# A two-layer diffusion block on one core: more buffers and an earlier load around the third stage, and the modulation beside Hyena and the second MLP moved from ScalarE and GpSimd to VectorE, its loads from SyncE's queue to GpSimd's

## The chip, the core and the metric

The kernel runs on one core of a Trainium2 chip. The metric is the device time of one execution in microseconds (us). TensorE (PE) multiplies, VectorE (DVE) and ScalarE (ACT) work on tiles elementwise, GpSimd (POOL) does a few elementwise operations and issues some DMAs, and SyncE (SP) issues the other DMAs. Each engine runs its own instructions in the order in which they stand in the program.

## The reference, cut to what matters

A block of two layers on 256 latent and 256 context tokens of 2048 channels, in float32. Layer 0 mixes tokens with a bidirectional RWKV-7 scan, layer 1 with a Hyena long convolution; each is followed by an MLP of width 8192. Six vectors a layer, made from the condition `c`, shift, scale and gate the streams. They are the modulation, and each is a matrix of 2048 x 2048 times a vector:

```python
mod = (silu_c @ ada_w[i] + ada_b[i]).reshape(B, N_MOD, 1, D)      # i = layer
h = modulate(rms_norm(x, norm_g[i, 0]), mod[:, 0], mod[:, 1])
y = rwkv_mixer(...)  if kind == 0 else  hyena_stream(h, ...)
x = x + mod[:, 2] * rms_norm(y, norm_g[i, 1])
h = modulate(rms_norm(x, norm_g[i, 2]), mod[:, 3], mod[:, 4])
x = x + mod[:, 5] * rms_norm(squared_relu_mlp(h, mlp_up[i], mlp_down[i]), norm_g[i, 3])
```

All of both layers' `ada_w` has to be loaded, 201 MB of float32, and the kernel spreads that over its stages.

## The kernel before, in words

**Precision.** A float32 operand is split into a high part (`wh`, `xh`: a cast on ACT) and a low part (`wl`, `xl`: a subtraction on DVE), and `mm3` makes three matmuls of them. A weight block of 1 MB is loaded by SP's queue into `w`, and each half of it costs one `wh` cast on ACT and one `wl` subtraction on DVE (`load_split`, `split_into`).

**Stages, in order of time.** (1) `start`, to 172 us: the first modulation and the mixes of the context and latent streams. (2) `rwkv_proj`, to about 440: the key projection `w_k`, with the second halves of the low-rank nets (`lora2`) beside it. After each block of keys `evk` copies it out (`kt`), squares it (`ksq`), splits the square (`ksh`, `ksl`) and sums it by heads on PE (line 783). (3) `rwkv_begin`, about 440 to 556, the third stage: the rest of `lora2`, `fill_r` and `fill_v` (projections of r and v, whose inputs `fx` are loaded by GpSimd's queue), and `scan_prepare(0)`, which makes the first scan group's operands (`KB`, `ard`, `Mn`, then an inversion in 31 pairs of `tmp` and `d`). (4) `rwkv_scan`, to about 1399. (5) `rwkv_out`, to 1475. (6) the first MLP, to 2245. (7) `hyena`, to about 2842: 24 pairs of column blocks of `hy_in_w` in the transposed layout, with `spectral` (transforms by matmul: `ud`, `pa`, `pb`, `ph`, `pl`) of one quarter of the channels beside the projections of the next, then `hy_out_w`, whose rows are evacuated as `y` and summed as `ysq`, and `resid`, which needs the factor `dg`. (8) the second MLP, to the end.

**`lora2`** makes 80 tiles in stages 2 and 3: three matmuls into `sc`, a tanh by ACT into `l2t`, a scaling of `l2t` by DVE or GpSimd, for 32 of them a scan by DVE into `l2u`, and a store of `l2t` or `l2u` to `scr` (`cum`, `a`, `gate`) by SP. A new `l2t` or `l2u` waits until the store of the tile that had its buffer has landed. In stage 3 its pool holds 3 buffers of each.

**The modulation.** `ada_first` and `ada_scan` put the vector through PE. `ada_run`, used in stages 2, 6, 7 and 8, multiplies a block of 128 rows by a scalar a row and adds it up: `acc += aw * s`, 16 blocks for 512 columns, then a matmul with `ones` and a small addition (`reduce`). The table `ONP` says for each stage which engines do it: with False, one DVE operation a block (`scalar_tensor_tensor`); with True, ACT scales `aw` in place and GpSimd adds it to `acc`. `ADA` says how many pieces of 512 columns a stage has: 16 in the first MLP, 8 in Hyena, 4 in the second MLP. A load `aw` holds one block beside Hyena (256 KB) and two beside the MLPs (512 KB), with two buffers; all of them are issued by SP. `ada_scan` loads its first `aw` when the scan begins.

**What sets the order.** The kernel is written as generators that take turns (`tick`, `beside`), and a scheduler of the framework then places each instruction by priority and by its own estimate of times; `high_priority` moves instructions ahead. So an edit can change the order on every engine. Pools set when a buffer is free again.

Of the kernel before, what the change touches and what calls it, by code (L numbers as in the profile page):

```python
# [10 lines left out]
F32 = mybir.dt.float32  # L11
F32R = mybir.dt.float32r
BF16 = mybir.dt.bfloat16
AF = mybir.ActivationFunctionType
# [55 lines left out]
class Kern:  # L70
# [233 lines left out]

    def ada_run(self, n, pool, psum="mm", on_pool=True, per=2, bufs=2, behind=None):


        nc = self.nc

        def reduce(layer, ch, i, acc):  # L310
            ps = getattr(self, psum).tile([P, 4, 2], F32, name=psum)
            for b in range(4):
                nc.tensor.matmul(ps[:, b, :], lhsT=acc[:, b * P : (b + 1) * P], rhs=self.ones[:, 0:2], start=True, stop=True)
            nc.vector.tensor_tensor(self.mod[:, layer, ch, 4 * i : 4 * i + 4], ps[:, :, 0],
                                    self.col("ada_b", layer * 96 + ch * 16 + 4 * i, 4), op=ALU.add)

        last = None
        for layer, ch, i in itertools.islice(self.ada_todo, n):
            acc = pool.tile([P, 512], F32, name="acc", bufs=per)
            c0 = ch * D + i * 512  # L320
            for k in range(0, KT, per):
                w = pool.tile([P, per, 512], F32, name="aw", bufs=bufs)
                with self.tc.issue_after(behind) if behind else ExitStack():
                    nc.sync.dma_start(w, self.I["ada_w"][layer, k * P : (k + per) * P, c0 : c0 + 512].rearrange("(a p) n -> p a n", p=P))
                for a in range(per):
                    s = self.sc2[:, 0, k + a : k + a + 1]
                    if on_pool:
                        nc.scalar.activation(w[:, a] if k + a else acc, w[:, a], AF.Identity, scale=s)
                        if k + a:
                            nc.gpsimd.tensor_tensor(acc, acc, w[:, a], op=ALU.add)  # L330
                    elif k + a == 0:
                        nc.vector.tensor_scalar(acc, w[:, a], s, None, op0=ALU.mult)
                    else:
                        nc.vector.scalar_tensor_tensor(acc, w[:, a], s, acc, op0=ALU.mult, op1=ALU.add)
                if k == 4 and per == 2 and last:
                    reduce(*last)
                yield
            last = layer, ch, i, acc
            if per == 1:
                yield  # L340
                reduce(*last)
        yield
        yield
        if last and per == 2:
            reduce(*last)

    def ada_scan(self, n, pool):
# [11 lines left out]
        todo = [(layer, ch, i, half, k4) for layer, ch, i in itertools.islice(self.ada_todo, n) for half in range(2) for k4 in range(4)]  # L359

        def load(u):
            layer, ch, i, half, k4 = todo[u]
            w = pool.tile([P, 4, 256], F32, name="aw", bufs=2)
            c0 = ch * D + i * 512 + half * 256
            nc.sync.dma_start(w, self.I["ada_w"][layer, k4 * 512 : (k4 + 1) * 512, c0 : c0 + 256].rearrange("(a p) n -> p a n", p=P))
            return w

        def finish(layer, ch, i, half, ps):
# [8 lines left out]

        nxt = load(0)
        tail = iter(())
# [16 lines left out]

    ONP = (False, False, False, True, True)
    ADA = (4, 8, 16, 8, 4)
# [298 lines left out]
    def lora2(self, pool):  # L697
# [33 lines left out]
        for q in range(4):  # L731
            for nm, e in (("dec", 0), ("dec", 1), ("a", 0), ("a", 1)):
                b0 = self.hw0 if nm == "dec" else self.ha0
                w = next(block)
                for j in range(4):
                    m = 4 * q + j
                    ps = self.sc.tile([P, 512], F32, name="sc")
                    self.mm3(ps, self.cut(w, slice(j * P, (j + 1) * P)), self.lora[nm, e], True, True)
                    t = self.l2p[0].tile([P, 512], F32, name="l2t")
                    nc.scalar.activation(t, ps, AF.Tanh, scale=0.5, bias=b0[:, e * 16 + m : e * 16 + m + 1])  # L740
                    (nc.gpsimd if m % 4 < self.LPOOL else nc.vector).tensor_scalar(t, t, 0.5, 0.5, op0=ALU.mult, op1=ALU.add)
                    if nm == "dec":
                        u = self.l2p[0].tile([P, 512], F32, name="l2u")
                        s = slice(None, None, -1 if e else 1)
# [4 lines left out]
        for q in range(8):  # L749
            w = next(block)  # L750
            for j in range(2):
                m = 2 * q + j
                ps = self.sc.tile([P, 512], F32, name="sc")
                for k in range(2):
                    self.mm3(ps[:, :L], self.cut(w, slice(k * 256 + j * P, k * 256 + (j + 1) * P)), self.lora["g", k], k == 0, k == 1)
                t = self.l2p[0].tile([P, 512], F32, name="l2t")
                nc.scalar.copy(t[:, :L], ps[:, :L])
# [3 lines left out]
    def rwkv_proj(self, l2, ad1):  # L761
# [11 lines left out]
        def evk(m, ps):  # L773
# [5 lines left out]
            sl = ev.tile([P, 512], F32R, name="ksl", bufs=1)  # L779
            nc.scalar.activation(s, ps, AF.Square, scale=self.col("k_k", m))  # L780
            self.split_into(sh[:], s[:], sl[:])
            for x in (sh, sl):
# [194 lines left out]
    def rwkv_scan(self, es, prep_pools, ngroups=KT // 2):  # L977
# [12 lines left out]
        ada = self.ada_scan(self.ADA[1], pool("ad", 2))  # L990
        self.bg, self.rate = [], 0.0
        with self.tc.high_priority(self.PRS):
            for i in range(2):
                self.scan_values(0, i)
# [749 lines left out]
    def run(self):  # L1744
        nc, tc = self.nc, self.tc
        with ExitStack() as es:
# [28 lines left out]
            with ExitStack() as e1:  # L1775
# [7 lines left out]
                for i, phase in enumerate((lambda: self.mlp(x, 0), lambda: self.hyena(x, (), 0), lambda: self.mlp(x, 1))):  # L1783
                    if self.upto >= 3 + i:
                        with ExitStack() as e2:
                            if self.ADA[2 + i]:
                                ad = self.pool(e2, "ad")
                                per = 1 if i == 1 else 2
                                ada = self.ada_run(self.ADA[2 + i], ad, "sg", self.ONP[2 + i], per)
                                if i == 1:  # L1790
# [97 lines left out]
```

## Time and profile before

| what | us |
|---|---|
| median of 3 runs (3551.66 to 3564.56) | 3557.94 |
| the profiled execution's own time | 3560.04 |
| its span, first to last instruction | 3558.3 |
| PE busy in the span | 3310.4 (93%) |
| DVE, ACT, POOL busy | 2453.0, 1749.9, 436.7 |

The page's chain of work that ended last follows back from the last instruction what released it. In the table by stretch, "PE busy" says how much of a stretch at least one matmul was in flight; since matmuls overlap, a stretch with PE busy for all of it has no wait left on PE. A wait names the instruction that waited, what ended the wait, the total in us, the count and the longest.

### The profile page before, as it was taken

The page shows a single profiled execution, that of the slowest core. Times are in us where ns is not written, and L with a number is a line of the kernel's source. Part 1 is how long each engine was busy: PE and PEld are TensorE (multiplying, and loading weights), DVE is VectorE, ACT ScalarE, POOL GpSimd, SP SyncE. Part 2 cuts the span into 40 slices and gives each one's busy share as a digit, 9 for nine tenths or more (in the row PEclk, how much of TensorE's full clock was granted, in tenths as well). Part 3 has the DMA queues.
Part 4 walks back from the last instruction along what each step waited for, and adds up shares of the span by engine and source line. Part 5 has one row for each costly group of instructions (what it writes and reads, how often), then busy time and mean ns, then how long its engine had stood idle before and what let it go on. Part 6 is the DMA issues. An engine that isn't in the chain of part 4 may idle for free.

```text
span 3558.3 us, 74568 instructions
## 1 busy us (share of the span) xinstructions
PE 3310.4 (93%) x30598; PEld 2894.7 (81%) x30598; DVE 2453.0 (69%) x3867; ACT 1749.9 (49%) x3070; POOL 436.7 (12%) x496
## 2 busy tenths in 40 slices
PE   6899888999899888899999999999999899999999
PEld 3477677887788766798989898899887798989897
DVE  4688776777777755687877776678786675555554
ACT  4454454555445444454444445566564663444343
POOL 0011121111111000000000002044441540000000
PEclk9899999999999989999999999999999999999999
DMA  9668898998888735688888886477665775555553
GB/s 309 203 224 285 261 343 271 290 282 262 259 268 262 227 122 186 201 272 280 284 296 281 298 265 228 160 224 227 213 204 179 241 256 189 178 189 189 189 180 129
DMA packets 587807, 836.79 MB, mean 235 GB/s; under 512 B 39551, under 2 KB 373280, under 8 KB 587464
## 3 DMA queue, kind: packets, MB, share of 16 engines
q1 hardware_dynamic: 556360, 718.76, 62.8%
q0 software_dynamic: 31104, 113.26, 10.2%
q8 instruction: 239, 3.92, 0.4%
q14 instruction: 104, 0.85, 0.1%
HBM read 777.31 MB, written 54.59 MB: 234 GB/s over the span
## 4 chain that ended last, share of the span: by engine, by line
PE 60%; DMA 16%; DVE 11%; ACT 5%; issue 4%; POOL 2%; SPq 1%; ACTq 0%; DVEq 0%; POOLq 0%
PE mm L112 45%; DMA aw<-in_ada_w 9%; PE sg L112 5%; PE fl L112 5%; PE sc L112 4%; POOL acc L330 2%; DVE tmp L53 1%; DVE wl L53 1%; DVE d L53 1%; ACT aw L53 1%; ACT wh L53 1%; DMA win<-in_window 1%; PE sc L414 1%; DMA cum<-cum 1%; PE sg L460 1%
## 5 line engine op out<-in xcount | busy, mean ns | idle before, releaser
L53 DVE TENSOR_TENSOR wl<-w,wh 128x1024 fp32r<-128x1024 f32 (+1 forms) x716 | 916.7, 1283 | 487.5 <-ACT wh L53 483.3
L53 ACT CAST wh<-w 128x1024 fp32r<-128x1024 f32 (+1 forms) x716 | 745.8, 1044 | 642.6 <-PE mm L112 578.7
L112 PE MATMUL mm<-hxh,wh 128*128 128x258 f32 x2816 | 801.1, 286 | 3.3 <-DVE nt L53 2.6
L112 PE MATMUL mm<-hxh,wl 128*128 128x258 f32 x2816 | 798.7, 284 | 3.8 <-DVE wl L53 3.6
L112 PE MATMUL mm<-hxl,wh 128*128 128x258 f32 x2816 | 797.9, 284 | 0.0
L112 PEld LDWEIGHTS mm<-hxh,wl 128*128 128x128 f32 x2816 | 532.3, 189 | 6.3 <-DVE wl L53 5.0
L112 PEld LDWEIGHTS mm<-hxh,wh 128*128 128x128 f32 x2816 | 532.8, 190 | 5.4 <-DVE nt L53 2.9
L112 PEld LDWEIGHTS mm<-hxl,wh 128*128 128x128 f32 x2816 | 535.1, 190 | 2.0 <-DVE hxl L53 0.2
L330 POOL TENSOR_TENSOR acc<-acc,aw 128x512 f32<-128x512 f32 x180 | 277.3, 1540 | 1325.9 <-PE mm L112 960.4
L112 PE MATMUL mm<-wh,uh 128*128 128x512 f32 x1024 | 403.0, 394 | 0.0
L112 PE MATMUL mm<-wh,ul 128*128 128x512 f32 x1024 | 401.0, 392 | 0.0
L112 PE MATMUL mm<-wl,uh 128*128 128x512 f32 x1024 | 398.5, 389 | 0.0
L53 DVE SCALAR_TENSOR_TENSOR acc<-aw,sc,acc 128x512 f32<-128x512 f32 x300 | 224.9, 750 | 98.6 <-DMA aw<-in_ada_w 96.1
L112 PEld LDWEIGHTS mm<-wh,ul 128*128 128x128 f32 x1024 | 192.1, 188 | 43.9
L112 PEld LDWEIGHTS mm<-wl,uh 128*128 128x128 f32 x1024 | 192.3, 188 | 41.8
L112 PE MATMUL fl<-fh,fx 128*128 128x256 f32 x1024 | 215.5, 297 | 11.3 <-DMA fx<-xv 9.8
L112 PEld LDWEIGHTS mm<-wh,uh 128*128 128x128 f32 x1024 | 192.4, 188 | 39.4
L53 ACT ACTIVATE aw<-aw,sc 128x512 f32<-128x512 f32 x180 | 125.9, 719 | 147.1 <-DMA aw<-in_ada_w 143.9
L112 PEld LDWEIGHTS fl<-fh,fx 128*128 128x128 f32 x1024 | 169.3, 194 | 29.0 <-issue 13.0
L112 PE MATMUL fl<-flo,fx 128*128 128x256 f32 x512 | 146.5, 286 | 0.0
L112 PE MATMUL sg<-ard,KB 64*64 64x64 f32 (+1 forms) x3584 | 130.5, 245 | 12.0 <-DVE NT L53 3.7
L112 PEld LDWEIGHTS sg<-ard,KB 64*64 64x64 f32 x3584 | 111.5, 137 | 18.3 <-DVE NT L53 4.7
(361 smaller groups left out, 5879.9 us busy)
## 6 DMA issues: line engine op xcount, KB each, us to landing
aw<-in_ada_w SPq DMA_DIRECT2D x288, 512.0 KB, 5.9
w<-in_mlp_down SPq DMA_DIRECT2D x128, 1024.0 KB, 5.3
w<-in_mlp_up SPq DMA_DIRECT2D x120, 1024.0 KB, 6.2
fx<-xv POOLq DMA_DIRECT2D x128, 512.0 KB, 6.3
aw<-in_ada_w SPq DMA_DIRECT2D x192, 256.0 KB, 3.7
w<-in_hy_in_w SPq DMA_DIRECT2D x44, 1024.0 KB, 5.3
fx<-xr POOLq DMA_DIRECT2D x64, 512.0 KB, 5.7
w<-in_w_k SPq DMA_DIRECT2D x16, 1024.0 KB, 7.7
```

Source lines behind the costliest of these rows:

```text
L53: return self.kern.pin(self.key, f(*a, **kw))
L112: return self.pin("pe", self.nc.tensor.matmul(out, lhsT=lhsT, rhs=rhs, **kw))
L330: nc.gpsimd.tensor_tensor(acc, acc, w[:, a], op=ALU.add)
L414: nc.tensor.matmul(ps[:, :n], lhsT=self.ones, rhs=sq[:, :n], start=acc is None and k == 0, stop=k == len(x) - 1)
L460: nc.tensor.matmul(pt[:, s], lhsT=y[k // 4, tt][:, k % 4 * P : (k % 4 + 1) * P], rhs=dg[:, tt], start=True, stop=True)
```

## The change

Five things change. `ada_scan` is cut in two, and its first `aw` load is issued when the scan's other pools are opened, at high priority, instead of after the scan's first values. `lora2`'s `l2t` gets 6 buffers and `l2u` 4 in stage 3, for 3 each (in stage 2 both keep 2). In `evk` the square and split of the last two key blocks get high priority. `ONP` becomes False for Hyena and the second MLP, so DVE does there what ACT and GpSimd did. In the same two stages the loads of `aw` are issued by GpSimd's queue.

```diff
-    def ada_run(self, n, pool, psum="mm", on_pool=True, per=2, bufs=2, behind=None):
+    def ada_run(self, n, pool, psum="mm", on_pool=True, per=2, bufs=2, behind=None, queue=None):
...
-                    nc.sync.dma_start(w, self.I["ada_w"][layer, k * P : (k + per) * P, c0 : c0 + 512].rearrange("(a p) n -> p a n", p=P))
+                    (queue or nc.sync).dma_start(w, self.I["ada_w"][layer, k * P : (k + per) * P, c0 : c0 + 512].rearrange("(a p) n -> p a n", p=P))
...
+        return self.ada_steps(pool, wide, pick, todo)
+
+    def ada_steps(self, pool, wide, pick, todo):
+        nc = self.nc
+
...
+        with self.tc.high_priority(self.PRS):
+            first = load(0)
+        yield
...
-        nxt = load(0)
+        nxt = first
...
-    ONP = (False, False, False, True, True)
+    ONP = (False, False, False, False, False)
...
-                    t = self.l2p[0].tile([P, 512], F32, name="l2t")
+                    t = self.l2p[0].tile([P, 512], F32, name="l2t", bufs=2 * self.l2p[1] + 2 * (self.l2p[1] > 1))
...
-                        u = self.l2p[0].tile([P, 512], F32, name="l2u")
+                        u = self.l2p[0].tile([P, 512], F32, name="l2u", bufs=2 * self.l2p[1])
...
-            nc.scalar.activation(s, ps, AF.Square, scale=self.col("k_k", m))
-            self.split_into(sh[:], s[:], sl[:])
+            with self.tc.high_priority(self.PRS if m >= KT - 2 else 0):
+                nc.scalar.activation(s, ps, AF.Square, scale=self.col("k_k", m))
+                self.split_into(sh[:], s[:], sl[:])
...
         ada = self.ada_scan(self.ADA[1], pool("ad", 2))
         self.bg, self.rate = [], 0.0
+        next(ada)
...
-                                ada = self.ada_run(self.ADA[2 + i], ad, "sg", self.ONP[2 + i], per)
+                                ada = self.ada_run(self.ADA[2 + i], ad, "sg", self.ONP[2 + i], per, queue=nc.gpsimd if i else None)
```

How it moves instructions at three places. **End of stage 2, ACT**: the squares of the last two key blocks (`ksq`, `ksh`) before `kt`, which begins the norm of the keys. Before:

```order
L53 ACTIVATE KB<-a,hka 128x512 x2
L53 ACTIVATE ksq<-mm,cols 128x512
L53 CAST fh<-fr 128x512
L53 CAST ksh<-ksq 128x512
L53 ACTIVATE ei<-cum 128x512
L53 ACTIVATE KB<-a,hka 128x512
L53 ACTIVATE ksq<-mm,cols 128x512
```

The program with the change has, on ACT at the same place:

```order
L53 ACTIVATE KB<-a,hka 128x512 x2
L53 ACTIVATE ksq<-mm,cols 128x512
L53 CAST fh<-fr 128x512
L53 CAST ksh<-ksq 128x512
L53 ACTIVATE ei<-cum 128x512
L53 ACTIVATE KB<-a,hka 128x512
L53 ACTIVATE ksq<-mm,cols 128x512
```

Nothing moved here: `KB`, which waits for a load of `a`, and the casts `fh` stand where they stood, and DVE and PE read alike up to the third stage too.

**End of stage 3, SP's queue**: the last loads and stores before the scan (`fr`: weights of r and v, `gate`: the last stores of `lora2`, `VU`: the scan's first values, `aw`: `ada_scan`'s loads). Before:

```order
L53 DMA fr<-in_w_v 128x2x256 x2
L53 DMA gate<-l2t 128x256 x2
L53 DMA VU<-v 64x128 x12
L53 DMA r<-fe 128x2x256
L53 DMA fr<-in_w_v 128x2x256 x3
L53 DMA aw<-in_ada_w 128x4x256 x2
```

With the change:

```order
L53 DMA gate<-l2t 128x256 x4
L53 DMA fr<-in_w_r 128x2x256
L53 DMA aw<-in_ada_w 128x4x256
L53 DMA v<-fe 128x2x256 x2
L53 DMA fr<-in_w_r 128x2x256 x2
L53 DMA VU<-v 64x128 x12
L53 DMA fr<-in_w_r 128x2x256 x2
L53 DMA fr<-in_w_v 128x2x256
L53 DMA aw<-in_ada_w 128x4x256
```

The first `aw` moved ahead of the twelve `VU` loads, the stores of `lora2` are through earlier, and the scan's first `w_v` load, which stood ahead of the `VU` loads, stands behind them.

**Middle of Hyena, DVE**: the spectral products `pa`, `pb`, `pl` between the weight splits `wl`. Before:

```order
L53 TENSOR_TENSOR pa<-sc,kk 128x512 x2
L53 TENSOR_TENSOR pb<-sc,kk 128x512
L53 TENSOR_TENSOR z<-mm,rstd 128x256
L53 TENSOR_TENSOR pa<-pa,pb 128x512
L53 TENSOR_TENSOR wl<-w,wh 128x1024
L53 TENSOR_TENSOR pb<-sc,kk 128x512
L53 TENSOR_TENSOR z<-mm,rstd 128x256
L53 TENSOR_TENSOR pl<-pa,ph 128x512
```

With the change:

```order
L53 TENSOR_TENSOR pa<-sc,kk 128x512 x2
L53 TENSOR_TENSOR pb<-sc,kk 128x512
L53 TENSOR_TENSOR z<-mm,rstd 128x256
L53 TENSOR_TENSOR mod<-sg,cols 128x4
L53 TENSOR_SCALAR acc<-aw,sc_92 128x512
L53 TENSOR_TENSOR pa<-pa,pb 128x512
L53 TENSOR_TENSOR wl<-w,wh 128x1024
L53 SCALAR_TENSOR_TENSOR acc<-aw,sc_92,acc 128x512
L53 TENSOR_TENSOR z<-mm,rstd 128x256
L53 TENSOR_TENSOR pb<-sc,kk 128x512
L53 SCALAR_TENSOR_TENSOR zc_29263<-z,cols,zc_29263 128x256
L53 TENSOR_TENSOR pl<-pa,ph 128x512
```

About one `acc` a `wl` came in, each of which waits on DVE for its load; ACT's scalings of `aw` and GpSimd's additions are gone from their queues, and GpSimd has the loads of `aw` in the additions' place, between its `z` memsets.

## Rows read from the trace of the kernel before

**Rows 1.** The page: busy time by engine, and the chain's shares by line.

```profile
PE 3310.4 (93%) x30598; PEld 2894.7 (81%) x30598; DVE 2453.0 (69%) x3867; ACT 1749.9 (49%) x3070; POOL 436.7 (12%) x496
...
PE mm L112 45%; DMA aw<-in_ada_w 9%; PE sg L112 5%; PE fl L112 5%; PE sc L112 4%; POOL acc L330 2%; DVE tmp L53 1%; DVE wl L53 1%; DVE d L53 1%; ACT aw L53 1%; ACT wh L53 1%; DMA win<-in_window 1%; PE sc L414 1%; DMA cum<-cum 1%; PE sg L460 1%
```

**Rows 2.** Busy time by stretch: length, engines' busy us (instructions), PE clock, DMA share, GB/s.

```profile
440.00:545.00 105.00, 86.94 (x872) 77.17 (x871) 80.42 (x146) 52.46 (x103) 26.79 (x41) 0.95 1.00 325
455.00:530.00 75.00, 62.53 (x490) 54.99 (x489) 60.07 (x114) 38.59 (x79) 20.83 (x31) 0.93 1.06 350
515.00:530.00 15.00, 12.19 (x95) 11.39 (x95) 13.55 (x32) 6.91 (x15) 2.69 (x5) 1.00 1.10 378
1600.00:2000.00 400.00, 400.00 (x2559) 364.55 (x2558) 316.62 (x434) 175.43 (x244) 0.00 (x0) 1.00 0.87 287
2340.00:2400.00 60.00, 58.55 (x458) 56.95 (x459) 50.51 (x65) 38.33 (x63) 23.74 (x22) 1.00 0.65 211
2400.00:2650.00 250.00, 232.30 (x1765) 222.34 (x1764) 195.84 (x252) 151.15 (x241) 107.56 (x98) 0.99 0.68 216
2650.00:2700.00 50.00, 48.28 (x266) 41.01 (x265) 45.26 (x61) 29.55 (x53) 12.46 (x11) 1.00 0.64 210
2842.00:2900.00 58.00, 58.00 (x485) 57.92 (x484) 44.67 (x49) 41.39 (x74) 38.38 (x25) 1.00 0.84 271
```

**Rows 3.** The chain through stage 3 in order of time: start, length, what.

```profile
477.64 8.16 DMA cum<-l2u
...
491.36 7.88 DMA a<-l2t
...
500.78 6.11 DMA a<-l2t
...
519.57 6.56 DMA gate<-l2t
...
556.44 7.35 DMA aw<-in_ada_w
```

**Rows 4.** Waits of PE from 420 to 600 us: total, count, longest.

```profile
PE sc L112 <- ACT l2t L53: 10.6, 8, 2.4
...
PE mm L112 <- DMA aw<-in_ada_w: 7.0, 1, 7.0
```

**Rows 5.** Groups on DVE in Hyena's middle, 2400 to 2650: busy, mean ns | idle before.

```profile
L53 DVE TENSOR_TENSOR wl<-w,wh 128x1024 fp32r<-128x1024 f32 x56 | 84.6, 1510 | 38.9 <-ACT wh L53 38.7
...
L53 DVE TENSOR_TENSOR pa<-pa,pb 128x512 f32<-128x512 f32 x20 | 22.1, 1106 | 0.1
L53 DVE TENSOR_TENSOR pl<-pa,ph 128x512 fp32r<-128x512 f32 x20 | 18.6, 932 | 2.3 <-ACT ph L53 2.3
```

**Rows 6.** The same groups from 2702 to 2745, where GpSimd adds next to nothing.

```profile
L53 DVE TENSOR_TENSOR wl<-w,wh 128x1024 fp32r<-128x1024 f32 x9 | 10.9, 1223 | 8.5 <-ACT wh L53 8.5
L53 DVE TENSOR_TENSOR pa<-pa,pb 128x512 f32<-128x512 f32 x4 | 2.7, 686 | 0.0
```

**Rows 7.** GpSimd's additions from 2400 to 2650.

```profile
L330 POOL TENSOR_TENSOR acc<-acc,aw 128x512 f32<-128x512 f32 x70 | 105.2, 1503 | 110.6 <-ACT aw L53 99.5 <-ACT acc L53 8.3 <-POOL acc L330 0.9
```

**Rows 8.** A wait of ACT from 2400 to 2650.

```profile
ACT aw L53 <- DMA aw<-in_ada_w: 77.2, 39, 6.2
```

**Rows 9.** The modulation on DVE beside the first MLP, 1600 to 2060.

```profile
L53 DVE SCALAR_TENSOR_TENSOR acc<-aw,sc,acc 128x512 f32<-128x512 f32 x175 | 130.8, 748 | 60.1 <-DMA aw<-in_ada_w 58.4
```

**Rows 10.** The page's DMA issues: engine, count, KB each, us to landing.

```profile
aw<-in_ada_w SPq DMA_DIRECT2D x288, 512.0 KB, 5.9
...
fx<-xv POOLq DMA_DIRECT2D x128, 512.0 KB, 6.3
```

**Rows 11.** GpSimd's issue of a load: ns min/median/max, first and last start.

```profile
L847 POOL DMA_DIRECT2D fx<-xv x128: 537/537/588, 454.5 to 1201.7; - x128
```

**Rows 12.** Waits of PE at Hyena's end, 2740 to 2842.

```profile
PE sg L460 <- DVE dg L53: 9.2, 1, 9.2
PE mm L112 <- DVE wl L53: 4.0, 4, 1.6
```

More of the change, by code (lines that the diff above doesn't have):

```diff
@@ L755, in lora2 @@
                     self.mm3(ps[:, :L], self.cut(w, slice(k * 256 + j * P, k * 256 + (j + 1) * P)), self.lora["g", k], k == 0, k == 1)
-                t = self.l2p[0].tile([P, 512], F32, name="l2t")
+                t = self.l2p[0].tile([P, 512], F32, name="l2t", bufs=2 * self.l2p[1] + 2 * (self.l2p[1] > 1))
                 nc.scalar.copy(t[:, :L], ps[:, :L])
```

## The prediction, as it stood before the run

> **What bounds the kernel now.** I read the page first: PE is busy for 93% of the span and heads the chain, but the second name in the chain is the load of `aw`, with 9% [rows 1]. A busy share of the whole span hides the stages, so the next view is the busy time by stretch [rows 2]. Beside the MLPs PE is busy for all of it (400.00 of 400 us from 1600 to 2000, 58.00 of 58 from 2842 to 2900), although the first has the modulation on DVE and the second has it on ACT and GpSimd: nothing that the modulation does there can be seen in the time. Two places are not like this. In the third stage (440 to 545) PE is busy for 86.94 of 105 us, while the DMA engines are busy all the time. In Hyena's middle (2400 to 2650) PE is busy for 232.30 of 250. So what the change is worth is decided at these two places, at the seam between stage 3 and the scan, and at Hyena's end. The chain and the waits at each place say what was late there.
>
> The sum is made against the profiled execution, 3560.0 us (span 3558.3 and 1.7 around it). That lies 2.1 above the median shown; I let this stand as rounding.
>
> **The change part by part.**
>
> *Priority of the last key squares: nothing.* PE does wait for `ksh` and `ksl` there, but the orders of ACT, DVE and PE are the same before and after up to the third stage; `KB` with its wait for a load still stands ahead of `ksq`. An edit that moves no instruction costs and gives 0.
>
> *First load of `ada_scan`: -4 us (0 to -7).* PE waits 7.0 us for this one load [rows 4]; it was issued at 556.44 and landed 7.35 later [rows 3]. Now it is issued ahead of the `VU` loads, which is before PE asks for it, so this wait goes. What is late next: the scan's first `w_v` weights, which PE takes right behind the modulation's matmul, have moved behind the twelve `VU` loads on SP's queue. They need a landing, a cast and a subtraction, so a part of the 7.0 may come back under their name. No row prices that; between none and all of 7.0 I take somewhat over half.
>
> *More buffers for `l2t` and `l2u`: -7 us (0 to -15).* The chain through stage 3 goes four times through a store that has to land before its buffer can be written again: 8.16, 7.88, 6.11 and 6.56 us, 28.7 together [rows 3]. With 6 and 4 buffers for 3 these steps leave the chain, and PE's 10.6 us of waits for ACT's `l2t` [rows 4] with them. The gain is not 28.7, because the DMA engines are what is late next: their share is 1.06 at 350 GB/s from 455 to 530, and the best 15 us reach 378 [rows 2]. The stage moves 105 us x 325 GB/s = 34.1 MB; at 350 this takes 97.5 us, 7.5 less, and at 378 it takes 90.3, 14.7 less. I take the first, since it is what the busy stretch held, and keep 0 and 15 as ends. DVE (80.42 of 105 busy) would allow this.
>
> *Modulation beside Hyena: -7 us (+26 to -32).* Removed, from 2400 to 2650: 70 additions by GpSimd [rows 7], the scalings by ACT, and ACT's 77.2 us of waiting in its queue for `aw` [rows 8], behind which stood the casts `wh`, `ph` and `uh`. DVE waits 38.7 us for `wh` there [rows 5]. Added on DVE: 70 blocks and some 5 first ones (one in 16) at 0.748 us, as beside the first MLP [rows 9], 56.1. Given back on DVE: while GpSimd adds, DVE's operations with two inputs in SBUF are longer, `wl` 1510 ns for 1223 and `pa<-pa,pb` 1106 for 686 [rows 5, 6]; with `pl` taken like the latter this is 56 x 0.287 + 20 x 0.420 + 20 x 0.246 = 29.4. DVE's work becomes 195.8 - 29.4 + 56.1 = 222.5 us, against PE's 232.3. Both can't run at 100%, because they feed each other. PE's 232.3 is the lower end: 17.7 less, and for the 450 us from 2300 to 2750 that is 17.7 x 1.8 = 32. For the other end I look how full DVE has been in this stage: 45.26 of 50 (0.905) at best, 50.51 of 60 (0.842) in another stretch where PE was nearly full [rows 2]. At 0.905 the 222.5 take 246, 4 less than 250, which makes -7; at 0.842 they take 264, and that is +26. I take the better share, because ACT, freed of its waits, will feed DVE earlier, and keep the other for the range. New is the wait for `aw` on DVE: behind it are queued `wl` and the products `pa` and `pl`, for which PE waits. Beside the first MLP DVE waits 58.4 us for 187 blocks [rows 9] with PE at 400 of 400, so such waits have been hidden, but with DVE 79% full and not 90%.
>
> *The queue of the loads: 0.* A GpSimd load of 512 KB lands in 6.3 us where SP's takes 5.9 [rows 10], and its issue takes 0.54 us of GpSimd's time [rows 11], which is free of 1.5 us additions now. SP no longer waits for `aw` buffers with weight loads behind it, but PE has hardly waited for a weight load in this stage. The Trainium skill (DMA: Bandwidth & Descriptors, Issuing engines are not separate DMA queues) says that DMAs of all issuing engines run on the same 16 DMA engines and that a second issuer saves sequencer time only. By this rule too the term is 0, and the 0.4 us between the two landing times agrees with it.
>
> *Hyena's end: -5 us (0 to -13).* PE waits 9.2 us for `dg` and 4.0 for `wl` from 2740 to 2842 [rows 12], since ACT, with the evacuations and casts in its queue, works through a ring of load, scaling and addition. In the new ring a block costs 0.75 us of DVE and no longer 0.7 of ACT and 1.5 of GpSimd, so it turns faster; but `dg` and `wl` are DVE's own, and the blocks now stand between them. I take under half of 13.2.
>
> *Second MLP: 0.* PE is full there before, and was full beside the first MLP with DVE doing this same work [rows 2, 9]. If DVE's cover failed, 40 blocks of 0.75, 30 us, would be exposed at most.
>
> Sum: -4 - 7 - 7 - 5 = -23; 3560 - 23 = **3537 us**.
>
> **The rivals.**
>
> *Nothing but the seam moves (3556).* For it: the DMA engines are at 1.00 in stage 3 already, and with more stores in flight each one takes longer; in Hyena DVE takes up what ACT loses and the 250 us stay 250. Against it: four waits for a single store in a row are latency, not throughput. 3560 - 4 = 3556.
>
> *DVE becomes Hyena's bound (3579, slower).* In Hyena each `acc` can stop DVE for a load while a `wl` or a `pl` waits behind it. If DVE gets no fuller than 0.842, Hyena costs +26; with half of stage 3's gain and the seam, 3560 - 4 - 3 + 26 = 3579. The point from which it decides: the stage gets longer when DVE's share stays under 222.5 / 250 = 0.89. For it speaks that most stretches are below that (195.84 of 250 is 0.78); against it, that 38.7 us of DVE's idle time there were waits for an ACT that is itself waiting [rows 5, 8].
>
> *PE's floor (3493).* All waits go: 3560 - 7 - 15 - 32 - 13 = 3493. Against it: the spectral chain from PE over DVE and ACT back to PE has waits of its own.
>
> *The loads on GpSimd's queue are held by DVE (3627).* A load that GpSimd issues would start only when the DVE operation that it meets is over. With 128 blocks beside Hyena, up to one `wl` of 1.22 us each [rows 6], and half of it absorbed by the second buffer, DVE stands still for 78 us more, and 3560 - 4 - 7 + 78 = 3627. The trace speaks against it: in the scan and in stage 3, with DVE at work, GpSimd's loads were issued in 537 ns at the median and 588 at most and landed like SP's [rows 10, 11]. The Trainium skill (SBUF — State Buffer, Summary: rules for kernel authors) advises against just this move: to hide a DMA of GpSimd's queue under DVE, issue it from ACT or SP, since DVE in its two-port modes keeps GpSimd from writing descriptors. Of two-input tensor_tensor operations, which most of Hyena's DVE work is, the same page (Who interferes with whom) says that they have no such mode.
>
> **How the numbers follow.** My forecast, 3515 to 3547, has 0.47. PE's floor or near it has 0.10, nothing but the seam 0.25, DVE as the bound 0.15, held loads 0.03. About 0.3% (10.7 us, here below 3547 or above 3569) is what a measurement of this kernel can tell from no change. So faster has 0.47 + 0.10 = 0.57, the same 0.25, slower 0.18. The range, 3505 to 3577, leaves out the held loads, most of the floor and half of the DVE case, together about 0.18.
>
> **What would show it.** Right: no wait of PE for `aw` at the scan's start; no store in the chain between 470 and 530, and DMA still near 1.0 there; `wl` at about 1.22 us in Hyena; DVE near 90% in Hyena's middle and PE above 93%. Wrong: DVE at 0.84 there with many waits of `acc` for `aw`, PE waiting for `wl` and `pl`; GpSimd issues well over 0.54 us; stage 3 as long as before; a wait for `fh` or `flo` at the scan's start that is as long as the 7.0.

## The result and the profile after

The changed kernel takes 3518.2 us (median; 3516.0 to 3520.2) against 3561.3 of the kernel before on the same chip: a ratio of 0.9891 (95% interval 0.9867 to 0.9914). In later runs beside other kernels (`after_again` below) it was 0.9874 (0.9856 to 0.9892). The forecast was 3537 in a range of 3505 to 3577: the sign and the range held, the gain of 43 us is nearly twice the 23 forecast.

The profiled execution took 3515.95 us with a span of 3513.1. On the page, the lines that answer to [rows 1], the loads of `aw` have fallen from 9% of the chain to 4%, ACT and GpSimd have less to do and DVE a little more:

```profile
PE 3290.9 (94%) x30598; PEld 2886.2 (82%) x30598; DVE 2474.5 (70%) x4059; ACT 1638.0 (47%) x2878; POOL 253.4 (7%) x476
...
PE mm L112 47%; DMA aw<-in_ada_w 4%; PE sg L112 4%; PE fl L112 4%; PE sc L112 3%; DVE tmp L53 1%; DVE d L53 1%; DVE wl L53 1%; DMA cum<-cum 1%; DMA fx<-xv 1%; DMA w<-in_hy_in_w 1%; DVE acc L53 1%; DMA win<-in_window 1%; DMA fr<-in_w_v 1%; PE sg L469 1%
```

Busy time by stretch of the kernel after, with the columns of [rows 2]; the first and the third start earlier than their counterparts by as much as the work there has moved forward, the other two lie somewhere in the same MLP:

```profile
435.00:540.00 105.00, 84.65 (x750) 74.83 (x750) 78.50 (x150) 52.18 (x102) 27.28 (x40) 0.93 1.00 322
1600.00:2000.00 400.00, 400.00 (x2526) 363.11 (x2525) 317.32 (x434) 174.38 (x238) 0.00 (x0) 1.00 0.88 290
2388.00:2638.00 250.00, 249.20 (x1892) 240.02 (x1891) 226.99 (x364) 124.02 (x199) 45.10 (x106) 1.00 0.73 236
2830.00:2890.00 60.00, 60.00 (x406) 55.60 (x405) 42.86 (x61) 28.67 (x45) 3.56 (x5) 1.00 0.73 239
```

The third row is the news: in Hyena's middle PE is busy for 249.20 of 250 us, where it was 232.30. The first row is the other: the third stage looks as it did.

To place the gain, I set marks at the same instruction in each trace: `kt`'s reciprocal (end of the second stage), the first product of the scan, the first load of `yt` (end of the scan), and the `dg` products that end the MLPs and Hyena. All lengths are in us of one profiled execution each; the last column is the ratio to the kernel before, from several runs. What each kernel is stands in the next section.

| kernel | start to `kt` | third stage | scan | first MLP | Hyena | second MLP | ratio (interval) |
|---|---|---|---|---|---|---|---|
| before | 439.6 | 115.4 | 829.8 | 763.4 | 545.8 | 744.4 | 1 |
| after | 434.4 | 115.1 | 822.3 | 764.1 | 512.3 | 743.4 | 0.9891 (0.9867–0.9914) |
| after_again | 435.7 | 115.6 | 818.4 | 766.1 | 510.2 | 742.9 | 0.9874 (0.9856–0.9892) |
| h_only | 434.5 | 118.6 | 823.2 | 760.9 | 511.3 | 743.9 | 0.9896 (0.9873–0.9919) |
| h_dve_sp | 436.2 | 116.5 | 824.4 | 763.4 | 511.5 | 743.8 | 0.9898 (0.9873–0.9923) |
| h_q | 434.3 | 115.5 | 828.8 | 761.1 | 558.2 | 745.7 | 1.0060 (1.0040–1.0079) |
| s3_only | 432.0 | 112.5 | 813.1 | 766.6 | 545.6 | 749.5 | 0.9986 (0.9969–1.0003) |
| first_only | 433.2 | 118.3 | 835.1 | 763.6 | 548.3 | 745.6 | 0.9996 (0.9980–1.0013) |
| buf_only | 434.6 | 121.8 | 826.8 | 760.8 | 545.6 | 745.9 | 0.9999 (0.9980–1.0017) |
| act_dve | 437.5 | 114.2 | 820.0 | 764.6 | 526.3 | 743.1 | 0.9942 (0.9922–0.9961) |
| no_add | 433.7 | 115.5 | 818.8 | 774.1 | 529.3 | 744.1 | 0.9941 (0.9923–0.9960) |
| half_fx | 434.5 | 115.1 | 788.5 | 765.5 | 508.8 | 742.8 | 0.9778 (0.9755–0.9801) |
| all_mlp1 | 434.6 | 112.8 | 823.9 | 810.6 | 503.8 | 739.1 | 0.9978 (0.9964–0.9993) |
| more_mlp1 | 436.2 | 116.3 | 823.1 | 864.0 | 496.8 | 738.8 | 1.0102 (1.0085–1.0119) |

From before to after Hyena gives 33.5 us of the span's 45.1, the scan 7.5, the stages up to `kt` 5.2 and the third stage 0.3. Not all of that is the change's: up to `kt` no instruction has moved on ACT, DVE or PE, and among the kernels of the table that stretch takes 432.0 to 439.6 whatever they change. Hyena's length repeats best: 545.6 to 548.3 in the four kernels with the old modulation, 508.8 to 512.3 in the five with the new one.

### The profile page after: what moved, and what is told of

Same layout as the page of the kernel before. It is cut to its first block, busy times and chain, and to the rows that moved or that the text cites. A ratio compares the mean times of both kernels' runs of the same rounds, so it can differ in the third digit from the quotient of the medians.

```text
span 3513.1 us, 74240 instructions
## 1 busy us (share of the span) xinstructions
PE 3290.9 (94%) x30598; PEld 2886.2 (82%) x30598; DVE 2474.5 (70%) x4059; ACT 1638.0 (47%) x2878; POOL 253.4 (7%) x476
## 4 chain that ended last, share of the span: by engine, by line
PE 60%; DMA 11%; DVE 8%; issue 5%; ACT 2%; SPq 1%; POOL 0%; DVEq 0%; POOLq 0%; ACTq 0%
PE mm L112 47%; DMA aw<-in_ada_w 4%; PE sg L112 4%; PE fl L112 4%; PE sc L112 3%; DVE tmp L53 1%; DVE d L53 1%; DVE wl L53 1%; DMA cum<-cum 1%; DMA fx<-xv 1%; DMA w<-in_hy_in_w 1%; DVE acc L53 1%; DMA win<-in_window 1%; DMA fr<-in_w_v 1%; PE sg L469 1%
## 5 line engine op out<-in xcount | busy, mean ns | idle before, releaser
L53 DVE TENSOR_TENSOR wl<-w,wh 128x1024 fp32r<-128x1024 f32 (+1 forms) x716 | 871.2, 1219 | 394.7 <-ACT wh L53 394.4
L53 DVE SCALAR_TENSOR_TENSOR acc<-aw,sc,acc 128x512 f32<-128x512 f32 x480 | 358.8, 748 | 156.6 <-DMA aw<-in_ada_w 153.6
L324 POOL DMA_DIRECT2D aw<-in_ada_w x160 | 91.6, 573 | 1464.2 <-ACT uh L53 954.6
L53 DVE TENSOR_TENSOR flo<-fr,fh 128x512 fp32r<-128x512 f32 x128 | 88.3, 690 | 66.3 <-ACT fh L53 53.0
L112 PE MATMUL mm<-xl,wh 128*128 128x512 f32 (+1 forms) x288 | 116.1, 403 | 11.4 <-DVE xl L53 11.4
```

The lines of the kernel that those rows point to most:

```text
L53: return self.kern.pin(self.key, f(*a, **kw))
L112: return self.pin("pe", self.nc.tensor.matmul(out, lhsT=lhsT, rhs=rhs, **kw))
L324: (queue or nc.sync).dma_start(w, self.I["ada_w"][layer, k * P : (k + per) * P, c0 : c0 + 512].rearrange("(a p) n -> p a n", p=P))
```

## The experiments

### Which half of the change carries it

`h_only` is the kernel before with the modulation's new form and its queue alone; `s3_only` has the other half alone (early first load of `ada_scan`, buffers, priority).

```
h_only, on the kernel before:
-    ONP = (False, False, False, True, True)
+    ONP = (False, False, False, False, False)
-  nc.sync.dma_start(w, self.I["ada_w"]...)
+  (queue or nc.sync).dma_start(w, self.I["ada_w"]...)
-  ada = self.ada_run(..., self.ONP[2 + i], per)
+  ada = self.ada_run(..., self.ONP[2 + i], per, queue=nc.gpsimd if i else None)
s3_only: the change without these lines
```

> The kernel before with the modulation's new form alone (one VectorE operation a block beside Hyena and the second MLP, loads by GpSimd's queue); the third stage and the first load of ada_scan stay as they were. In the trace Hyena, from one set of dg products to the next, went from 545.8 to 512.3 us, and the span from 3558.3 to 3513.1. Theory 'Hyena carries it, the rest is a real gain of the third-stage parts': this kernel has Hyena's -33 alone, about 3528 (ratio 0.9906). Rival 'the third-stage parts give nothing, and what is missing is variation from one execution to the next': it is as fast as the whole change, 3518 (0.988).

> The kernel before with the other half alone: first load of ada_scan early, more buffers for l2t and l2u, priority of the last key squares; the modulation beside Hyena and the second MLP is as before. Theory 'the third-stage parts are a real gain': about 3551 (ratio 0.997), with the scan's start 5 us earlier and the scan 7 us shorter. Rival 'they give nothing, because fx and rx loads took the stores' place in the third stage and a wait for ACT took that of the load at the scan's start': 3561 (1.000), and the marks before and after the scan move by no more than those of two executions of the kernel before.

`h_only` has 0.9896, as good as the whole change within the intervals; `s3_only` has 0.9986 with 1 just inside its interval. So the modulation carries the gain, and the third-stage half is worth 5 us with a margin of 6 either way: it can't be told from nothing. The interval of `h_only` holds the ratios of both of its theories, 0.9906 and 0.988, so it doesn't choose between them; its Hyena is 34.5 us shorter and its ratio is worth 37.

### The two edits of the third-stage half, one by one

```
first_only: only ada_steps with its early load, and next(ada) ahead of the VU loads
buf_only:   only bufs=... for l2t and l2u
```

> The kernel before with only the first load of ada_scan issued early. The half change with all three third-stage edits had a ratio of 0.9986 (0.9969 to 1.0003), -5 us. Theory 'the early load is what is worth something there': 0.9986, with PE's wait for aw at the scan's start gone and the scan shorter than the 653 to 657 us that it took (start of the scan to the last fl) in four kernels without the edit. Rival 'nothing': 1.000 and 653 to 657 us.

> The kernel before with only the additional buffers for l2t and l2u. Theory 'the buffers give nothing, since the DMA engines are full in the third stage and loads take the stores' place in the chain': 1.000, third stage (from kt's reciprocal to the scan's start) 115 to 119 us as in the four kernels without the edit. Rival 'they give the -5 us of the half change': 0.9986 and a third stage of 110 to 113 us.

Both are at 1.000. For `buf_only` the theory of no gain holds; its third stage, at 121.8, is the longest of all and even above the 115 to 119 expected. Over the table the stage takes 116.9 us on average in the five kernels without the buffers (115.4 to 118.6) and 115.4 in the nine with them (112.5 to 121.8): a microsecond or two may be there, the 7 of the prediction are not. For `first_only` the waits of PE at the scan's start, over the same 50 us in each kernel, show what the early load does. In `h_only`, which has the late load (total, count, longest):

```profile
PE mm L112 <- DMA aw<-in_ada_w: 8.6, 1, 8.6
```

In `first_only`:

```profile
PE sg L112 <- DVE KB L53: 2.3, 1, 2.3
PE mm L112 <- DMA aw<-in_ada_w: 2.2, 1, 2.2
```

In the kernel after:

```profile
PE sc L112 <- ACT rhs L53: 5.2, 1, 5.2
PE fl L112 <- DMA fx<-xv: 1.4, 1, 1.4
```

With the late load the wait is 7.0, 8.4, 8.6 and 8.8 us in four kernels (in `buf_only` 4.9, under the name of `pick`); with the early one it is 2.2 or gone, and a wait for ACT of 5.2, 3.1 or 1.3 us (after, `s3_only`, `after_again`) has come in its place. That nets some 2 to 7 us at this one point. The whole time doesn't resolve it.

### What the third stage is bound by

The prediction held that behind the stores the DMA engines' throughput comes next. `half_fx` takes bytes away.

```
 def fill_x(self, src):
-    self.nc.gpsimd.dma_start(x, src)
+    self.nc.gpsimd.dma_start(x[:, 0], src[:, 0])
 and x[:, 0] in the place of x[:, 1] in fill_v and fill_r
```

> The changed kernel with only the first half of each fx tile loaded (256 KB instead of 512 KB) and used in the place of the second; PE, VectorE and ACT do as much as before, and the second halves are left out of the sum. In the third stage 28 such loads stand, so 7.3 of its 34.2 MB go, which at the 325 GB/s of the stage are 22 us. Theory 'the DMA engines' throughput bounds the third stage, so that stores that leave the chain are replaced by loads': third stage (kt's reciprocal to the scan's start) 93 to 103 us, where kernels with and without the change had 112.5 to 121.8. Rival 'something else is late there, PE's chain or the latency of single transfers': 108 us or more.

The third stage took 115.1 us, exactly as long as in the kernel after. The 105 us of the first row by stretch above, in `half_fx`:

```profile
435.00:540.00 105.00, 84.84 (x768) 75.89 (x767) 79.91 (x151) 53.23 (x103) 29.75 (x42) 0.94 0.91 275
```

The DMA engines moved 275 GB/s instead of 322 and PE and DVE did the same work in the same time. So my theory of that experiment falls: neither the stores' latency (`buf_only`) nor the bytes set this stage's length. What does, I did not settle. PE and DVE are busy for 85 and 80 of 105 us, and the chain of `half_fx` through the stage is made of many short pieces of DVE, ACT and PE between single loads, which fits a chain of dependent steps; no run tested that. One such chain can be read in the traces: the inversion, whose `tmp` and `d` take turns on DVE, starts at 494, 496 and 489 us (before, after, `half_fx`) and takes 44, 43 and 45 us, so neither the buffers nor the bytes shortened it.

### The operation or the queue

`h_dve_sp` is the kernel before with only the operation changed (the line `ONP`); `h_q` only with the queue changed (the two edits on `queue`), so that ACT scales and GpSimd adds as before.

> The kernel before with only the operation changed: one VectorE operation a block beside Hyena and the second MLP, but the loads stay on SP's queue. Theory 'the queue is worth nothing, PE did not wait for weight loads': as h_only. Rival 'SP, which waits for a free aw buffer with weight loads queued behind it, holds the weights up': between h_only and the kernel before, 5 to 20 us slower than h_only, with waits of PE or ACT for w in Hyena.

> The kernel before with only the queue changed: ACT scales and GpSimd adds as before, but the loads are issued by GpSimd, in order between its additions. Theory 'the queue is worth nothing': 3561 (1.000). Rival 'the loads now stand behind additions of 1.5 us and their waits for ACT': the ring turns more slowly, Hyena's tail gets longer and the time rises by 5 to 20 us.

`h_dve_sp` is as `h_only`, 0.9898 against 0.9896, with Hyena at 511.5 against 511.3: beside the new operation the queue is worth nothing. Beside the old one it costs: `h_q` is 0.6% slower and Hyena 12 us longer. Where GpSimd itself adds, a load stands in order behind its additions; here is one row by stretch for all of Hyena, the last busy time being GpSimd's. Before:

```profile
2254.00:2800.00 546.00, 504.82 (x3489) 466.61 (x3489) 410.28 (x530) 325.69 (x531) 199.39 (x173) 0.98 0.65 210
```

`h_q`:

```profile
2247.00:2805.00 558.00, 509.88 (x3488) 471.84 (x3488) 405.53 (x528) 323.32 (x526) 249.71 (x289) 0.96 0.63 204
```

GpSimd is busy for 50 us more, with the issues of the loads (121 take 68.5 us), and they lie in the ring of load, scaling and addition. The time goes late, as the rival said: from 50 us after Hyena's start `h_q` does 2630 matmuls in 374 us and the kernel before 2633 in 372, and what is left of Hyena takes 134 us against 124.

### GpSimd's additions or ACT's waits

Two things went from beside Hyena at once: GpSimd's additions, which lengthened DVE's operations, and ACT's scalings with their waits. `act_dve` puts ACT's scaling back and lets DVE add; `no_add` puts it back and leaves the additions out. In both GpSimd still issues the loads.

```
 on the kernel after: ONP[3] = True (beside Hyena), and
-   nc.gpsimd.tensor_tensor(acc, acc, w[:, a], op=ALU.add)
+   nc.vector.tensor_tensor(acc, acc, w[:, a], op=ALU.add)     (act_dve)
+                                                              (no_add: no line)
```

> The changed kernel with ACT scaling each block beside Hyena again, as in the kernel before, and VectorE (not GpSimd) adding it. The loads, ACT's scalings and ACT's waits for aw in its queue are there again; GpSimd's additions are not. Hyena from dg to dg was 545.8 us before and 512.3 after; VectorE's wl took 1452 ns before and 1217 after over this stretch. Theory 'GpSimd's additions, which lengthen VectorE's two-input operations, cost the 33 us': Hyena 511 to 518, wl 1.22 us. Rival 'ACT's waits for aw, with the casts wh, ph and uh behind them, cost them': Hyena 535 to 546 with wl at 1.22 us all the same.

> The changed kernel with ACT scaling each block beside Hyena again and nobody adding: the additions beside Hyena are left out, so the time is that of a kernel without them. ACT's scalings and its waits for aw stay, GpSimd adds nothing and VectorE has no block to do. Theory 'GpSimd's additions cost the 33 us': Hyena 508 to 514, which is PE's floor. Rival 'ACT's waits cost them': Hyena stays at 530 to 546 although VectorE is free of both.

Hyena took 526.3 and 529.3 us, between the two theories. Without GpSimd's additions DVE's `wl` is at 1219 and 1222 ns again, and Hyena is shorter by 16.5 us (`no_add`) to 19.5 (`act_dve`) of the 33.5; the other 14 to 17 go only when ACT's part, its scalings and its waits together, goes too. But the two kernels lose them at different places. Here is the stretch of about 2630 of Hyena's 3489 matmuls that begins some 50 us after its start, with the columns of [rows 2]. Before:

```profile
2304.00:2676.00 372.00, 348.21 (x2633) 332.47 (x2633) 298.11 (x379) 234.98 (x385) 161.52 (x148) 0.99 0.69 220
```

After, then `act_dve`, then `no_add`:

```profile
2292.00:2630.00 338.00, 336.27 (x2629) 327.37 (x2627) 302.63 (x486) 173.45 (x278) 60.71 (x148) 1.00 0.74 240
2294.00:2634.00 340.00, 339.89 (x2631) 329.76 (x2630) 293.68 (x465) 228.38 (x368) 56.09 (x140) 1.00 0.74 237
2304.00:2657.00 353.00, 343.20 (x2634) 332.00 (x2634) 245.36 (x383) 226.03 (x371) 54.53 (x137) 0.99 0.69 222
```

`act_dve` has nearly the whole gain here, 32 of 34 us, with ACT's scalings and 49.3 us of its waits for `aw` still there. It loses its 14 us almost all behind this stretch, in the last quarter's spectral chain: PE waits 5.1 us for one `pa` there, additions that wait for ACT's `aw` stand among the products on DVE, and the granted clock is 0.85 from 2645 to 2680. `no_add` loses 15 of its 17 us in the stretch itself, with 96.2 us of ACT's waits for `aw`, and nothing behind it. That it isn't faster than `act_dve`, although DVE has 105 additions less to do, shows that DVE's work isn't what is left there. So it is shown that taking GpSimd's additions away is worth 16.5 to 19.5 us with ACT's part still there. What ACT's part costs by itself is not shown: its price differs between the two kernels, no run took it away and kept GpSimd's additions, and none takes its scalings and its waits apart. ACT's waits for `aw` in Hyena, before:

```profile
ACT aw L53 <- DMA aw<-in_ada_w: 107.8, 58, 6.2
```

In `act_dve`:

```profile
ACT aw L53 <- DMA aw<-in_ada_w: 67.3, 47, 4.9
```

In `no_add`:

```profile
ACT aw L53 <- DMA aw<-in_ada_w: 104.1, 59, 4.5
```

What DVE's `wl` waits for stands in its group over all of Hyena (count | busy, mean ns | idle before): in `no_add` 89.7 us for the cast `wh`, which is in ACT's queue behind such waits, in `act_dve` 35.2, and in the kernel after 25.0. `no_add`:

```profile
L53 DVE TENSOR_TENSOR wl<-w,wh 128x1024 fp32r<-128x1024 f32 x130 | 158.5, 1222 | 90.0 <-ACT wh L53 89.7
```

The kernel after, with other groups that are needed below:

```profile
L53 DVE TENSOR_TENSOR wl<-w,wh 128x1024 fp32r<-128x1024 f32 x130 | 158.1, 1217 | 25.0 <-ACT wh L53 25.0
L53 DVE SCALAR_TENSOR_TENSOR acc<-aw,sc,acc 128x512 f32<-128x512 f32 x129 | 96.2, 746 | 33.8 <-DMA aw<-in_ada_w 33.2
L53 DVE SCALAR_TENSOR_TENSOR zc<-z,cols,zc 128x256 f32<-128x256 f32 x96 | 44.3, 476 | 0.1
L53 DVE TENSOR_TENSOR pa<-pa,pb 128x512 f32<-128x512 f32 x32 | 21.8, 682 | 0.1
L53 DVE TENSOR_TENSOR pl<-pa,ph 128x512 fp32r<-128x512 f32 x32 | 21.8, 681 | 0.9 <-ACT ph L53 0.7
```

The wait for the load has moved with the operation, from ACT (107.8 us) to DVE (33.2). On DVE it is a third as long, and PE is busy for 249.20 of 250 us in Hyena's middle all the same.

### Where a block on DVE stops being free

The second MLP's and half of Hyena's modulation, moved beside the first MLP, where PE is full and DVE is busy for 581 of 764 us:

```
-    ADA = (4, 8, 16, 8, 4)
+    ADA = (4, 8, 20, 8, 0)        (all_mlp1)
+    ADA = (4, 8, 24, 4, 0)        (more_mlp1)
```

> The changed kernel with the four columns of modulation that ran beside the second MLP moved beside the first (counts 4, 8, 20, 8, 0 in the place of 4, 8, 16, 8, 4). In the trace after, five of these blocks stood on VectorE between the last y of Hyena and dg, and PE waited 10.6 us for dg. Theory 'the blocks are part of that wait and the first MLP has room for them (VectorE busy for 581 of 764 us with PE full)': the wait for dg 6 to 8 us, Hyena 508 to 510, the first MLP 763 to 766 as before, ratio to the kernel before about 0.988, 3 to 5 us under the changed kernel. Rival 'the wait is that for the last weights' load, cast and subtraction': dg waits 10 us all the same, 3516.

> The changed kernel with counts 4, 8, 24, 4, 0: half of Hyena's modulation beside the first MLP too. Theory 'PE is at its floor in Hyena's middle already and VectorE has room beside the first MLP': as the kernel with counts 4, 8, 20, 8, 0, or up to 5 us under it from Hyena's spectral chain, whose waits for VectorE get shorter. Rival 'VectorE gets full beside the first MLP (581 of 764 us, and 128 blocks of some 0.7 more make 670) and PE waits there': the first MLP 770 us or more, no gain.

> The changed kernel as it is, beside the others on the same chip: 0.989 of the kernel before; third stage 112 to 119 us, Hyena 511 to 513 us.

The kernel after (`after_again`) came out much as expected beside them, with Hyena at 510.2 us. At Hyena's end the theory held: PE's longest wait in Hyena, for the last `dg`, fell from 10.6 us in the kernel after

```profile
PE sg L469 <- DVE dg L53: 13.9, 2, 10.6
```

to 6.9 in `all_mlp1`,

```profile
PE sg L469 <- DVE dg L53: 10.2, 2, 6.9
```

and Hyena is at 503.8. But the first MLP got 46.5 us longer for 64 blocks, and 99.9 for 128: 0.73 and 0.78 us a block, about its length on DVE (0.75). Here are the first MLP's row by stretch and DVE's two largest waits in it. After:

```profile
1478.00:2242.00 764.00, 754.05 (x4832) 688.21 (x4832) 581.34 (x808) 338.24 (x497) 9.82 (x20) 0.99 0.82 268
```

```profile
DVE acc L53 <- DMA aw<-in_ada_w: 94.7, 57, 3.7
DVE wl L53 <- ACT wh L53: 63.7, 68, 2.4
```

`all_mlp1`:

```profile
1480.00:2290.00 810.00, 774.01 (x4864) 697.64 (x4864) 619.91 (x875) 328.69 (x496) 10.01 (x20) 0.99 0.84 273
```

```profile
DVE acc L53 <- DMA aw<-in_ada_w: 154.3, 85, 4.7
DVE wl L53 <- ACT wh L53: 22.4, 24, 1.9
```

DVE's idle time there was no room. A block that waits for its load holds DVE, which runs in order, as a busy one does: 581 + 95 = 676 of 764 us were taken. The 64 blocks added 39 us of work and 60 of waiting; 41 of that came out of the time in which DVE had waited for ACT, 10 out of its waits for `o`, `mod` and `nt`, and the remaining 48 are, but for rounding and small waits, the 46 by which the stage grew. This is an account of DVE's time and not yet a cause. PE's largest waits in `all_mlp1` are those for DVE:

```profile
PE mm L112 <- DVE wl L53: 14.8, 18, 2.0
PE mm L112 <- DVE nt L53: 12.5, 12, 2.2
```

So both kernels lose to the kernel after, and my theory of room beside the first MLP falls. A second explanation stands beside a full DVE, and no run takes the two apart: beside the first MLP SP issues the `aw` loads, with the loads of weights in order behind them. In the kernel after ACT's casts waited 2.6 us for this MLP's weights, in `all_mlp1` 130.6:

```profile
ACT wh L53 <- DMA w<-in_mlp_down: 69.7, 19, 6.3
ACT wh L53 <- DMA w<-in_mlp_up: 60.9, 15, 6.6
```

The same kernel with the first MLP's `aw` loads on GpSimd's queue would tell. No kernel here that does the whole work beats the changed kernel measurably. Hyena itself gained little by the lighter load: 64 blocks less, from `all_mlp1` to `more_mlp1`, shortened it by 7.0 us, 0.11 a block.

## Why the prediction was half right

**Key squares, 0.** No instruction moved, and no run shows anything to charge to it.

**First load, -4 (0 to -7).** The wait for `aw` of [rows 3, 4] is gone, and a part came back, as the step said, though under another name: not `fh` or `flo` but ACT's `rhs`, 1.3 to 5.2 us. The scan, in which this point lies, takes 826.6 us on average in the four kernels without any of the three edits (823.2 to 829.8) and 819.9 in the seven with all three and whole loads (813.1 to 823.9), which agrees with a few microseconds; `first_only`, at 835.1, does not (its profiled execution, 3570.2, was the longest of its twelve). It stays open.

**Buffers, -7 (0 to -15): the step that failed.** The stores of [rows 3] did leave the chain, as foretold. The chain of the kernel after through the same stretch (start, length, what) holds loads in their place:

```profile
480.58 8.45 DMA rx<-r
...
495.22 5.79 DMA fx<-xv
...
510.24 5.88 DMA fx<-xv
...
519.23 6.13 DMA fx<-xr
...
527.46 6.14 DMA fx<-xr
```

Together they last 32.4 us, the four stores 28.7, and the stage is as long as it was. The step took the stores' time as removable and the throughput of the DMA engines as what comes next, at 350 GB/s. `half_fx` refutes the second half, `buf_only` the first, each by the profile of one execution. A chain names the one path that ended last; it does not say how far ahead the next one ended. My sign for "right" (no store in the chain, DMA near 1.0) came true without a gain, so it was no test.

**Beside Hyena, -7 (+26 to -32): the mechanism was right in part, the term mis-sized.** With the tail Hyena gave 33.5, where -7 and -5 stood. Two numbers in DVE's sum were off, both the same way. First, what GpSimd's additions lengthen: I counted `wl`, `pa` and `pl` and left out `zc`, which also has two inputs in SBUF. Over all of Hyena the groups before were

```profile
L53 DVE TENSOR_TENSOR wl<-w,wh 128x1024 fp32r<-128x1024 f32 x130 | 188.3, 1452 | 93.0 <-ACT wh L53 92.7
L53 DVE SCALAR_TENSOR_TENSOR zc<-z,cols,zc 128x256 f32<-128x256 f32 x96 | 61.6, 647 | 8.8 <-ACT zc L53 7.3
L53 DVE TENSOR_TENSOR pa<-pa,pb 128x512 f32<-128x512 f32 x32 | 31.5, 983 | 0.2
L53 DVE TENSOR_TENSOR pl<-pa,ph 128x512 fp32r<-128x512 f32 x32 | 29.0, 907 | 3.0 <-ACT ph L53 2.9
```

and the same rows after, above, have 30.2, 17.3, 9.7 and 7.2 us less: 64.4, of which 17.3 were not in the sum. Second, the added blocks were taken at their length, 0.748 us, and set against a busy time by stretch, in which overlapping ends count once. A block starts the next instruction 0.66 us after itself (DVE in order of time, after: start, length, what):

```profile
2503.26 0.74 DVE L53 SCALAR_TENSOR_TENSOR acc<-aw,sc,acc 128x512 f32<-128x512 f32 x1
2503.92 0.69 DVE L53 TENSOR_TENSOR pa<-pa,pb 128x512 f32<-128x512 f32 x1
```

DVE's busy time over Hyena so rose from 410.28 to 427.33, 17 us. The row by stretch after:

```profile
2242.00:2755.00 513.00, 493.11 (x3489) 461.63 (x3490) 427.33 (x668) 246.23 (x395) 74.64 (x171) 0.98 0.69 224
```

The work that took PE 232.3 of 250 us before costs DVE 226.99 x 232.3 / 249.20 = 211.6 us now, where the sum had 222.5. At my own share of 0.905 that is 234 us, hence PE's floor: the share that I took as reachable was reached (226.99 of 250 is 0.908), it was the work that I had too high. What a sum over DVE can't hold shows in `no_add`: DVE is busy for 245.36 of 353 us in its stretch, 0.70, and the stretch is still 15 us longer than after. The waits in ACT's queue had no term of their own, only a say in the choice of the share. The rival of PE's floor named the right mechanism in this one place, -32 with all waits gone, and I gave it 0.10. The rival of DVE as the bound did not come here, but it may have come beside the first MLP in `all_mlp1`.

**The queue, 0.** Right: `h_dve_sp` against `h_only`. The rival of loads held by DVE didn't come true: GpSimd's 125 issues in Hyena took 537 ns at the median and 732 at most, with DVE busy for 0.908 of the time:

```profile
L324 POOL DMA_DIRECT2D aw<-in_ada_w x125: 537/537/732, 2284.4 to 2754.8; - x125
```

**Hyena's end, -5 (0 to -13).** PE's wait for `dg` grew from 9.2 to 10.6 us and that for `wl` fell from 4.0 to 0.5, 2.1 us together. The row of [rows 12] after, from 2695 to 2797:

```profile
PE sg L469 <- DVE dg L53: 10.6, 1, 10.6
PE mm L112 <- DVE wl L53: 0.5, 1, 0.5
```

The step named the reason against itself, that blocks would stand ahead of `dg`: six of them ran on DVE while PE waited (the expectation of `all_mlp1` says five behind the last `y`; three of the six stand there). Without them the wait is 6.9.

**Second MLP, 0.** Right: 744.4 and 743.4 us, PE full. With no modulation beside it, in `all_mlp1` and `more_mlp1`, it took 739.1 and 738.8, so either form costs some 4 us there, which a PE busy for all of a stretch doesn't show.

So of the terms Hyena is -33.5 for -12, the third stage 0 for -7, the seam a few microseconds for -4. What remains of the 43 us, some 5 up to `kt`, lies in the part that the change doesn't touch, and in the spread of single executions. That the total came no further from the forecast is partly luck: the buffers' 7 us that did not come offset a third of what Hyena gave beyond its terms.

## What to carry to other kernels

When an operation moves off a helper engine, add up everything that the helper had slowed: each operation of the same kind of operands, and each queue that waited on its behalf; here the additions alone made 16.5 to 19.5 of 33.5 us, and the rest came only with ACT's part gone too. Set durations against busy time only when both count overlaps alike. Idle time of an in-order engine is room for more work only as far as it isn't waits for loads, and as the queue that issues the loads has room too: the same block cost 0.11 us in one stage and 0.73 in another whose DVE was 76% busy.

## What the runs showed of the hardware

GpSimd's additions lengthened DVE operations that read both inputs from SBUF: `wl` 1452 ns for 1217, `zc` 647 for 476, `pa<-pa,pb` 983 for 682, `pl` 907 for 681. `pb<-sc,kk`, whose one input comes from PSUM, took 683 before and 681 after. That it is the additions and not ACT's scalings is shown by `act_dve`, which has the scalings: 1219, 477, 682 and 682 ns. The Trainium skill (SBUF — State Buffer, Who interferes with whom) says that a DVE instruction with two SBUF inputs contends with a GpSimd instruction that reads SBUF; these rows agree.

Not expected either: taking 256 KB off each `fx` load left the third stage alone, where the DMA engines' share was 1.00, and shortened the scan from 822.3 to 788.5 us, where their share was 0.80. In the scan PE was busy for 726.65 us instead of 743.55 with the same matmuls, at a granted clock of 0.97 instead of 0.95, and idle for 17 us less; only 8.2 us of its waits after were for `fx` by name. What it relieved there stays open.
